# The last two down products of the second block exchanged, and the last row block finished in halves

## The chip, the cores and the metric

The kernel runs on one core of a Trainium2 chip. The core has TensorE for matrix products, VectorE, ScalarE and GpSimd for everything element by element, and SyncE, which issues most transfers; the profile calls them PE (PEld for its weight loads), DVE, ACT, POOL and SP. Each engine takes its instructions in order and waits for the others by semaphores. TensorE writes its sums into PSUM, eight banks of 128 x 512 float32 values; everything else lies in SBUF or in device memory. The metric is the device time of one execution in microseconds (us), as the median of several runs.

## The reference

The program is an encoder of two layers over 1024 tokens of width 1024. Each layer is a token mixer and a gated feed-forward block, each followed by a layer norm:

```python
for i in range(DEPTH):
    mix = _mla_mixer(h, ...) if i % 2 == 0 else _diff_mixer(h, ...)
    h = _layernorm(ALPHA * h + mix, ln_mix_g[i], ln_mix_b[i])
    h = _layernorm(ALPHA * h + _swiglu(h, ffn_w_gu[i], ffn_w_down[i]), ln_ffn_g[i], ln_ffn_b[i])

def _swiglu(x, w_gu, w_down):
    gate, up = jnp.split(x @ w_gu, 2, axis=-1)
    return (jax.nn.silu(gate) * up) @ w_down
```

The layer norm takes each row's mean and variance over its 1024 values, with the variance as the mean of the squares about the mean. Here only the last step matters: the product with `w_down` (2816 x 1024) of the second layer, the addition to the residual, and the last layer norm, whose result is the output.

## The kernel before

**The down product.** `ffn` (L486) computes the gated block for one layer; the second layer calls it with `next_x` None (L1388). The matrix product with `w_down` is done in Winograd's form of Strassen's scheme: rows are cut into two halves (row blocks 0 to 3 and 4 to 7, of 128 tokens each), columns into two halves of 512, the inner size into two halves of 11 blocks of 128, and seven products of half size take the place of eight. Each product pairs one of seven combinations of h, written to device memory earlier (`h_dr`), with a combination of weight quarters made on the fly. In the code's names, with the weights they use, the order before is b11, t1, b21, t2, b22, t3, t4 (L817 to L879). b11, b21 and b22 are quarters of the weights as loaded; t1 to t4 are differences, which VectorE subtracts first (for t4 at L769).

**One product** has 11 steps j. A step takes one 128 x 512 block of h and one of the weights, each split into a high part (ScalarE copies it, L469) and a low part (the difference, L470: VectorE for h, GpSimd for weights). `step` (L779) then issues three matmuls (high by high, high by low, low by high) for one row block t, so a whole product is 11 x 4 x 3 = 132 matmuls of 512 columns. `whole` (L787) goes over j outside and t inside.

**Banks.** Two sets of four PSUM banks are used in turn, `x4` and `y4`, one bank for each t. A product either begins anew in its banks or goes on adding to what is there: t3 adds onto t2, and t4 onto both, all in y4, because the scheme wants t2, t2 + t3 and t2 + t3 + t4. After each product `added` (L796, issued at L798) lets VectorE add the banks to the right quarter of the result z. A bank that is read there can be written by TensorE only when VectorE is done. b22 lies in x4, between t2 and t3.

**Operands.** Split blocks of h and of weights take their places in turn from three sets of slots, `wh` (3), `wl` (3) and `o` (6): twelve in all (`op_unit`, L474). Only t4 of this layer differs: its weights go to the eleven `tt` tiles (L775), which held the upper half of the raw weights until then, so that all of its h and weights can be kept. Raw h comes in groups of four blocks through two buffers (L725), raw weights in groups of four through larger ones; `load_down` (L715) keeps all these loads in the program's order on SP.

**The end before.** t4's steps go over row blocks 0 and 1 together, step by step; then come all eleven steps of row block 2, then those of row block 3 (L866 to L879). Behind each row block stand `added` and `finish`.

**The layer norm** (`layer_norm`, L163) of a row block: VectorE forms minus the mean in two scalings (L166, L167) from two sums that `added` collected; ScalarE squares both halves about the mean with a running sum (L170); VectorE centres and multiplies by the gain (L176); it adds the two sums of squares (L178); GpSimd raises that to -1/2 (L180); VectorE multiplies and adds the bias (L183); SP stores (L184). The very last row block does the final step and the store in two halves of 512 columns. Row blocks 4 to 7 are finished after b22, while TensorE works on t3.

**Order.** The lines above are in program order. A scheduler at build time takes that order as the priority, simulates the engines, and lays each engine's queue out from it; so an instruction that the simulation finds ready earlier can stand ahead of one that the program lists first. `behind` (L155) pins one instruction after another: t4's subtractions from the third on stand behind the last `added` before them (L771).

## Time and profile before

| | us |
|---|---|
| median of three runs | 2318.11 (2317.43 to 2320.41) |
| the profiled execution | 2317.24 |
| its span, first to last instruction | 2315.5 |
| VectorE busy in the span | 1560.1 |
| ScalarE busy in the span | 1018.5 |
| GpSimd busy in the span | 891.9 |

The profile is of one execution. Its page gives each engine's busy time and share; the other views are lists. In the timeline a row has the start in us from the span's beginning, the duration, the engine, the line of the kernel, the operation, the tiles (written <- read), the shape, how many were merged (x), and in brackets how long the engine sat idle before and what ended that. A matmul's duration includes the time in which it drains, so that matmuls overlap: their pace is the distance of starts. The view by windows has a row for each stretch: its length, then the busy time and number of instructions of PE, PEld, DVE, ACT and POOL, the clock granted to TensorE as a share of full speed, the share of time that the transfer engines were busy, and GB/s. Groups by line give busy time, the mean of one in ns, and idle time before. The chain lists the work that ended last, step by step. Tile names: op_h and op_w are split operands, wt the split weights in the tt tiles, dx, dy, dw and dv the banks of the products, z the result, fg and fb the gain and bias.

### The profile page before, as it was taken

The numbers are of one execution on the slowest core, as the hardware profiler recorded it, in microseconds if no ns is written. First come the engines' busy times: TensorE is split into PE (matmuls) and PEld (weight loads), VectorE is DVE, ScalarE is ACT, GpSimd is POOL, SyncE is SP. The second block draws the span as 40 slices with busy tenths as digits, with TensorE's granted clock in tenths as the row PEclk, the third lists the DMA queues.
The fourth block names the chain that finished last, engine by engine and source line by source line (L and its number), as shares of the span: only waits on it lengthen the run. The fifth ranks groups of instructions, "written<-read, shape, count | busy, mean of one in ns | idle before, by whom it ended". The sixth has DMA issues, their size and how long they took to land. (4 is left out here: it accounts for less than half of the span.)

```text
span 2315.5 us, 31126 instructions
## 1 busy us (share of the span) xinstructions
PE 2253.4 (97%) x11410; PEld 1918.7 (83%) x11410; DVE 1560.1 (67%) x2879; ACT 1018.5 (44%) x2092; POOL 891.9 (39%) x698
## 2 busy tenths in 40 slices
PE   9999999999999999999999999979999999999997
PEld 9898897888888887888888898967778888887886
DVE  5666664596666658677476766666596656658777
ACT  4466673352332324345465656545442333324343
POOL 2233351014444445465332423222014444436564
PEclk9999999999999999999999999989999999999999
DMA  5121335334323238454310202153344222337453
GB/s 202 41 91 69 106 101 178 125 142 145 125 76 129 86 119 322 182 183 140 101 46 31 71 25 69 37 191 111 126 144 149 99 103 102 113 129 303 146 203 121
DMA packets 103658, 288.29 MB, mean 125 GB/s; under 512 B 8528, under 2 KB 31696, under 8 KB 93008
## 3 DMA queue, kind: packets, MB, share of 16 engines
q1 hardware_dynamic: 98064, 268.46, 33.0%
q0 software_dynamic: 5440, 17.83, 2.3%
q8 instruction: 90, 1.47, 0.3%
q14 instruction: 64, 0.52, 0.1%
HBM read 205.00 MB, written 77.07 MB: 122 GB/s over the span
## 5 line engine op out<-in xcount | busy, mean ns | idle before, releaser
L469 ACT CAST op_g<-gr 128x512 fp32r<-128x512 f32 x240 | 147.5, 622 | 411.0 <-PE gb L514 228.3
L470 POOL TENSOR_TENSOR op_g<-gr,op_g 128x512 fp32r<-128x512 f32 x104 | 145.8, 1407 | 303.6 <-DVE tmp L605 153.6
L470 DVE TENSOR_TENSOR op_h<-rh,op_h 128x512 fp32r<-128x512 f32 x154 | 162.8, 1088 | 67.6 <-ACT op_h L469 67.6
L514 PE MATMUL ga<-xh_m,op_g 128*128 128x512 f32 x512 | 168.0, 389 | 0.0
L469 ACT CAST op_h<-rh 128x512 fp32r<-128x512 f32 x154 | 93.0, 619 | 145.0 <-PE dx L782 37.5
L782 PE MATMUL dw<-op_w_t,op_h 128*128 128x512 f32 x660 | 151.4, 390 | 0.0
L782 PEld LDWEIGHTS dw<-op_w_t,op_h 128*128 128x128 f32 x660 | 123.6, 188 | 25.9 <-DVE op_h L470 0.4
L222 ACT ACTIVATE l_b<-l_b,mx_b 128x256 f32<-128x256 f32 (+7 forms) x128 | 99.6, 778 | 76.2 <-DVE mx_b L219 74.2
L1281 POOL TENSOR_SCALAR l_b<-l_b,r_b,cst 128x128 f32<-128x128 f32 (+3 forms) x64 | 52.8, 825 | 205.1 <-DVE r_b L224 196.1
L470 POOL TENSOR_TENSOR op_w_t<-tt,op_w_t 128x512 fp32r<-128x512 f32 x66 | 98.8, 1501 | 77.1 <-ACT op_w_t L469 77.1
L782 PE MATMUL dx<-op_w_b,op_h 128*128 128x512 f32 x528 | 122.7, 392 | 5.9 <-ACT op_w_b L469 3.9
L782 PEld LDWEIGHTS dx<-op_w_b,op_h 128*128 128x128 f32 x528 | 98.3, 188 | 29.9 <-ACT op_w_b L469 4.7
L514 PE MATMUL gb<-t4h_f,op_g 128*128 128x512 f32 x352 | 115.8, 390 | 3.0 <-DVE tmp L597 3.0
L514 PE MATMUL gc<-b22h_f,op_g 128*128 128x512 f32 x352 | 115.6, 389 | 1.6 <-ACT op_g L469 1.6
L470 DVE TENSOR_TENSOR op_g<-gr,op_g 128x512 fp32r<-128x512 f32 x136 | 109.5, 807 | 9.0 <-ACT op_g L469 8.8
L514 PE MATMUL gc<-t1h_f,op_g 128*128 128x512 f32 x352 | 115.5, 389 | 0.0
L514 PE MATMUL gb<-t3h_f,op_g 128*128 128x512 f32 x352 | 115.2, 389 | 0.0
L514 PE MATMUL gb<-t2h_f,op_g 128*128 128x512 f32 x352 | 114.8, 389 | 0.0
L514 PEld LDWEIGHTS ga<-xh_m,op_g 128*128 128x128 f32 x512 | 96.1, 188 | 19.9
L470 POOL TENSOR_TENSOR op_g<-s,op_g 128x512 fp32r<-128x512 f32 x40 | 55.3, 1382 | 143.6 <-ACT op_g L469 143.6
L143 PE MATMUL bp<-xT_f,h_wb 128*128 128x512 f32 x256 | 103.4, 404 | 0.0
L145 PE MATMUL bp<-xT_f,l_wb 128*128 128x512 f32 x256 | 101.8, 398 | 0.0
(375 smaller groups left out, 6788.4 us busy)
## 6 DMA issues: line engine op xcount, KB each, us to landing
gr<-in_w_gu SPq DMA_DIRECT2D x44, 1024.0 KB, 6.7
rh<-h_dr SPq DMA_DIRECT2D x28, 1024.0 KB, 5.3
h_dr<-sh SPq DMA_DIRECT2D x22, 1024.0 KB, 4.9
h_dr<-hp SPq DMA_DIRECT2D x22, 768.0 KB, 4.1
tt<-in_w_dn SPq DMA_DIRECT2D x22, 512.0 KB, 7.5
rh<-h_dr SPq DMA_DIRECT2D x14, 768.0 KB, 4.3
z<-xs_dr SPq DMA_DIRECT2D x16, 512.0 KB, 10.0
rw_b<-in_w_dn SPq DMA_DIRECT2D x8, 1024.0 KB, 8.7
```

The lines of the kernel that those rows point to most:

```text
L143: T.matmul(ps_out, lh, rh, start=(i == 0), stop=False)
L145: T.matmul(ps_out, ll, rh, start=False, stop=(i == n - 1))
L222: A.activation(l[:, :n], l[:, :n], AF.Exp, bias=mx, scale=-1.0, accum_out=sm)
L469: A.copy(hi, src)
L470: eng.tensor_tensor(lo, src, f32(hi), ALU.subtract)
L514: T.matmul(o, w[:, a, kc], x[b][:, k, :], start=(first and k == 0 and (a, b) == (0, 0)), stop=(k == 3 and a == 1), skip_group_check=True,)
L782: T.matmul(o, h[:, a, c], w[:, b_], start=(first and (a, b_) == (0, 0)), stop=(last and a == 1), skip_group_check=True,)
L1281: G.tensor_scalar(l1[:, :n], l1[:, :n], r1, nlam, ALU.mult, ALU.mult)
```

## The change

In the second layer b22 moves from between t2 and t3 to the very end. The products now run b11, t1, b21, t2, t3, t4, b22: t2, t3 and t4 follow each other on y4, and t4 is an ordinary `whole` product whose weights take the common slots. Row blocks 0 to 3 are finished after t4; b22's split weights are put into the tt tiles, its steps go over row blocks 4 and 5 together, then 6, then 7, and each is finished behind its steps. For row block 7 the first half of the result is complete much earlier (after b21), and `last_row_block` squares that half about its own mean ahead of time; `end` squares the second half about the same mean and corrects by the square of the difference of the two means. It also centres the two halves separately, so that the second half's centring stands behind the request for the power -1/2, and writes the result in three stores: the first 512 columns by SP, the next 256 by ScalarE's queue, the last 256 by SP. `layer_norm` loses its parameter for halves. The first layer keeps its order (`third`).

```diff
-    def layer_norm(z, sums, junk, y, g, b, name, dst, n=1):
+    def layer_norm(z, sums, junk, y, g, b, name, dst):
...
-        for i in range(n):
-            c = slice(i * D // n, (i + 1) * D // n)
-            V.scalar_tensor_tensor(y[:, c], y[:, c], rs, b[:, c], ALU.mult, ALU.add)
-            nc.sync.dma_start(dst[:, c], y[:, c])
+        V.scalar_tensor_tensor(y, y, rs, b, ALU.mult, ALU.add)
+        nc.sync.dma_start(dst, y)
...
-                if next_x is not None:
-                    yield unit(r, f"t4_{j}", G, ("o",))
-                    continue
-                t = poolx.tile([P, 2, 512], F32R, tag=f"tt{j}", name=f"wt4{layer}_{j}")
+                yield unit(r, f"t4_{j}", G, ("o",)) if next_x is not None else unit(r, f"t4_{j}")
+
+        def b22_kept():
+            for j, r in enumerate(w_block(1, hi_half, "b22")):
+                t = poolx.tile([P, 2, 512], F32R, tag=f"tt{j}", name=f"wt{layer}_{j}")
                 split((t[:, 0], t[:, 1]), r, G)
                 yield t
...
+        def last_row_block(tb, o, junk):
+            s_lo, s_hi = (sums[tb][:, i:i + 1] for i in range(2))
+            nb, q = small(f"nb{layer}"), small(f"q{layer}")
+            sq, d, nmu, rs = (small(f"{k}{layer}", 2) for k in ("sq", "dm", "nm", "rs"))
+
+            def square(i, cs, to):
+                A.activation(to, z[tb][:, cs], AF.Square, bias=nb, scale=1.0 / 32, accum_out=sq[:, i:i + 1])
+
+            V.tensor_scalar(nb, s_lo, -1.0 / (32 * 512), None, ALU.mult)
+            square(0, lo_half, junk)
+            V.tensor_scalar(q, sq[:, 0:1], LN_EPS, None, ALU.add)
+
+            def end():
+                added(0, hi_half, o, tb - 4, 1)
+                square(1, hi_half, o)
+                V.tensor_scalar(nmu[:, 0:1], s_hi, s_lo, -1.0 / D, ALU.add, ALU.mult)
+                V.tensor_scalar(d[:, 0:1], s_hi, s_lo, 1.0 / D, ALU.subtract, ALU.mult)
+                V.tensor_scalar(d[:, 1:2], d[:, 0:1], d[:, 0:1], -1.0, ALU.mult, ALU.mult)
+                V.tensor_scalar(d[:, 1:2], d[:, 1:2], q, None, ALU.add)
+                y, dst = z[tb], x_dst[tb * P:(tb + 1) * P, :]
+                V.scalar_tensor_tensor(y[:, lo_half], y[:, lo_half], nmu[:, 0:1], g[:, lo_half], ALU.add, ALU.mult)
+                V.tensor_scalar(rs[:, 1:2], sq[:, 1:2], d[:, 1:2], None, ALU.add)
+                G.tensor_tensor(rs[:, 0:1], rs[:, 1:2], mhalf[:, 0:1], ALU.pow)
+                V.scalar_tensor_tensor(y[:, hi_half], y[:, hi_half], nmu[:, 0:1], g[:, hi_half], ALU.add, ALU.mult)
+                for cs, eng in ((lo_half, nc.sync), (slice(512, 768), nc.scalar), (slice(768, 1024), nc.sync)):
+                    V.scalar_tensor_tensor(y[:, cs], y[:, cs], rs[:, 0:1], b[:, cs], ALU.mult, ALU.add)
+                    eng.dma_start(dst[:, cs], y[:, cs])
+
+            return end
...
+        def third():
+            whole(x4, from_h(6, "3"), block(1, hi_half, "b22"), True)
+            for t in range(4):
+                added(0, hi_half, x4[t], t, 1)
+                finish(4 + t, [x4[t], x4[t]])
+
         x4 = accumulators("v", "x")
-        whole(x4, from_h(6, "3"), block(1, hi_half, "b22"), True)
-        for t in range(4):
-            added(0, hi_half, x4[t], t, 1)
-            finish(4 + t, [x4[t], x4[t]])
+        if next_x is not None:
+            third()
...
         if next_x is None:
+            whole(y4, from_h(2, "4"), t4(), False)
+            for t in range(4):
+                added(1, lo_half, y4[t], t, 0)
+                finish(t, [y4[t], y4[t]])
+            end = last_row_block(7, x4[3], y4[3])
             hs, ws = [], []
-            for h, w in zip(from_h(2, "4"), t4()):
+            for j, (h, w) in enumerate(zip(from_h(6, "3"), b22_kept())):
                 hs.append(h)
                 ws.append(w)
                 for t in range(2):
-                    step(y4[t], h, w, t, False, len(hs) == 11)
+                    step(x4[t], h, w, t, j == 0, j == 10)
+            for t in range(4):
+                if t > 1:
+                    for j in range(11):
+                        step(x4[t], hs[j], ws[j], t, j == 0, j == 10)
+                if t == 3:
+                    end()
+                else:
+                    added(0, hi_half, x4[t], t, 1)
+                    finish(4 + t, [x4[t], x4[t]])
             stx.close()
-            last(0)
-            last(1)
-            for t in range(2, 4):
-                for j in range(11):
-                    step(y4[t], hs[j], ws[j], t, False, j == 10)
-                last(t)
```

More of the change, by code (lines that the diff above doesn't have):

```diff
@@ L804, in finish @@
             y = z[tb] if y is None else y
-            return layer_norm(z[tb], sums[tb], junk, y, g, b, f"{nm}_{tb}", x_dst[tb * P:(tb + 1) * P, :],
-                              2 if next_x is None and tb == 3 else 1)
+            return layer_norm(z[tb], sums[tb], junk, y, g, b, f"{nm}_{tb}", x_dst[tb * P:(tb + 1) * P, :])
+        def last_row_block(tb, o, junk):
[23 more added lines that the diff above has]
+            return end
         def accumulators(name, tag):
@@ L859, in ffn @@
             added(1, hi_half, y4[t], t, 1)
-        def last(t):
-            added(1, lo_half, y4[t], t, 0)
-            finish(t, [y4[t], y4[t]])
         new, rest, normed = None, [], []
         if next_x is None:
+            whole(y4, from_h(2, "4"), t4(), False)
[3 more added lines that the diff above has]
+            end = last_row_block(7, x4[3], y4[3])
             hs, ws = [], []
-            for h, w in zip(from_h(2, "4"), t4()):
+            for j, (h, w) in enumerate(zip(from_h(6, "3"), b22_kept())):
                 hs.append(h)
```

## The prediction

> **What bounds the kernel now.** I read the page first, then the last four stages by window, then the timeline around the end, then the last part of the chain.
>
> ```profile
> span 2315.5 us, 31126 instructions
> PE 2253.4 (97%) x11410; PEld 1918.7 (83%) x11410; DVE 1560.1 (67%) x2879; ACT 1018.5 (44%) x2092; POOL 891.9 (39%) x698
> 2210.70:2240.80 30.10, 30.10 (x134) 24.74 (x133) 21.96 (x21) 15.41 (x28) 23.17 (x16) 1.00 0.46 167
> 2240.80:2270.80 30.00, 30.00 (x133) 24.59 (x131) 29.18 (x42) 18.36 (x38) 16.92 (x13) 1.00 0.59 210
> 2270.80:2303.80 33.00, 30.62 (x133) 24.62 (x132) 25.90 (x40) 11.88 (x23) 15.87 (x11) 1.00 0.18 65
> 2303.80:2315.50 11.70, 0.00 (x0) 0.00 (x0) 6.56 (x12) 1.87 (x6) 1.09 (x2) 0.71 0.34 135
> ```
>
> The program is bound by TensorE: 97% of the span, and in the three windows (one each for the b22, t3 and t4 products; the fourth is the tail) it is busy throughout, but for the last, where 33.00 us hold 30.62 of work. The tail, 11.70 us, has no matmul. So the change can save in two places only: the holes of the t4 product and the tail. Everything earlier in the program stays as it is. The profiled execution took 2317.24 us, its span and 1.74 around it; the median of the runs is 2318.11, 0.87 above it. I subtract from the median.
>
> The holes, in the timeline:
>
> ```profile
> 2244.66 26.23 PE L782 MATMUL dw<-op_w_t,op_h 128*128 128x512 f32 x115
> 2268.05 0.32 SPq L717 DMA_DIRECT2D rh<-h_dr  x1
> 2271.54 0.68 DVE L798 SCALAR_TENSOR_TENSOR z<-z,dw 128x512 f32<-128x512 f32 x1
> 2272.37 1.63 PE L782 MATMUL dw<-wt,op_h 128*128 128x512 f32 x6 [1.48 <-DVE z L798]
> 2272.83 1.66 ACT L469 CAST op_h<-rh 128x512 fp32r<-128x512 f32 x3 [6.19 <-DMA rh<-h_dr]
> 2273.48 0.69 DVE L470 TENSOR_TENSOR op_h<-rh,op_h 128x512 fp32r<-128x512 f32 x1 [1.25 <-ACT op_h L469]
> 2274.09 0.68 DVE L798 SCALAR_TENSOR_TENSOR z<-z,dw 128x512 f32<-128x512 f32 x1
> 2274.83 15.52 PE L782 MATMUL dw<-wt,op_h 128*128 128x512 f32 x67 [0.83 <-DVE z L798]
> 2289.74 13.99 PE L782 MATMUL dw<-wt,op_h 128*128 128x512 f32 x61
> ```
>
> The first row gives the pace: 115 matmuls in 26.23 us, the last taking 0.39, so (26.23 - 0.39) / 114 = 0.2267 us each, and 132 x 0.2267 = 29.92 per product. t3's last matmul ends at 2270.89, t4's at 2303.73: 32.84, so **2.92 us** were lost. t4 adds into the banks y4 that t3 filled, and VectorE must read a bank before TensorE writes it again. The read of the first bank (2271.54) and of the second (2274.09) came late because VectorE's queue held split operands of h ahead of them, and one of these waited for ScalarE's copy, which waited 6.19 us for an h load issued at 2268.05.
>
> The tail:
>
> ```profile
> 2299.00 0.69 DVE L798 SCALAR_TENSOR_TENSOR z<-z,dw 128x512 f32<-128x512 f32 x1 [0.33 <-PE dw L782]
> 2304.08 0.69 DVE z L798 x2
> 2304.69 1.28 DVE L176 SCALAR_TENSOR_TENSOR z<-z,nmu_f,fg 128x1024 f32<-128x1024 f32 x1
> 2306.01 0.21 DVE L166 TENSOR_SCALAR nmu_f<-fs 128x1 f32<-128x1 f32 x1
> 2306.13 0.21 DVE L167 TENSOR_SCALAR nmu_f<-fs 128x1 f32<-128x1 f32 x1
> 2306.25 0.69 ACT L170 ACTIVATE dw<-z,nmu_f 128x512 f32<-128x512 f32 x1 [2.21 <-DVE nmu_f L166]
> 2306.88 0.19 ACT L170 ACTIVATION_READ_ACCUMULATOR dw<-z,nmu_f 128x1 f32 x1
> 2306.76 1.28 DVE L183 SCALAR_TENSOR_TENSOR z<-z,rs_f,fb 128x1024 f32<-128x1024 f32 x1 [0.42 <-POOL rs_f L180]
> 2307.96 1.28 DVE L176 SCALAR_TENSOR_TENSOR z<-z,nmu_f,fg 128x1024 f32<-128x1024 f32 x1
> 2309.15 0.21 DVE L178 TENSOR_SCALAR ve_f<-ssq_f 128x1 f32<-128x1 f32 x1
> 2309.44 0.55 POOL L180 TENSOR_TENSOR rs_f<-ve_f,cst 128x1 f32<-128x1 f32 x1 [2.72 <-DVE ve_f L178]
> 2310.03 1.41 DVE L183 SCALAR_TENSOR_TENSOR z<-z,rs_f,fb 128x512 f32<-128x512 f32 x2 [0.66 <-POOL rs_f L180]
> 2310.80 0.99 SPq L184 DMA_DIRECT2D out_dram<-z  x2
> out_dram<-z SPq DMA_DIRECT2D x2, 256.0 KB, 2.0
> ```
>
> From the last matmul's end (2303.73) to the first of the final two VectorE halves (2310.03; call it F) are **6.30 us**; from F to the end of the span 5.47, of which 1.41 are the two halves and 2.0 the last store's landing. In the 6.30, VectorE still works off the row block before the last (2304.69, 2306.76: 1.20 us apart from their followers each), so that the last one's mean comes at 2306.01, 1.24 us after its sums (2304.08 + 0.69 = 2304.77), and its centring pass (2307.96) behind another wide pass.
>
> **Part 1: the products exchanged.** Before, b22 (other banks) lay between t2 and t3, and its 30 us hid VectorE's reads of t2's banks. Now t2, t3, t4 follow each other on y4, so there are two transitions on one bank, and t4 to b22 changes banks and needs no wait. Behind a late read all of TensorE stands. What such a transition costs is read where VectorE's order was undisturbed, at b22's end:
>
> ```profile
> 2224.72 16.25 PE L782 MATMUL dv<-op_w_b,op_h 128*128 128x512 f32 x71
> 2238.97 0.69 DVE L798 SCALAR_TENSOR_TENSOR z<-z,dv 128x512 f32<-128x512 f32 x1 [2.05 <-PE dv L782]
> 2239.58 1.77 DVE L470 TENSOR_TENSOR op_h<-rh,op_h 128x512 fp32r<-128x512 f32 x1
> 2241.27 0.68 DVE L798 SCALAR_TENSOR_TENSOR z<-z,dv 128x512 f32<-128x512 f32 x1
> 2242.13 0.67 DVE L798 SCALAR_TENSOR_TENSOR z<-z,dv 128x512 f32<-128x512 f32 x1
> 2242.73 0.67 DVE L798 SCALAR_TENSOR_TENSOR z<-z,dv 128x512 f32<-128x512 f32 x1
> ```
>
> b22's last matmul ends at 2240.97, so the next would start at 2240.81. Its reads end at 2239.66, 2241.95, 2242.80 and 2243.40. Had the next product used these banks, three matmuls (0.68) for each bank in turn: the first at 2240.81, the second held from 2241.49 to 2241.98, the third from 2242.66 to 2242.83, the fourth from 2243.51 not at all: 0.65 us, and the first six after a hole take 0.1 longer (1.63 at 2272.37, against 5 x 0.2267 + 0.39 = 1.52): **0.75** each, 1.5 for two. The bounds: 0 each when no operand is queued between the reads, 2.92 each as at the t4 product now. I take 1.5, since the h load that came late belonged to a product whose eleven weights had tiles of their own and whose h filled all slots ahead; now t3 loads no weights, t4's h and weights share twelve slots and are prepared six pairs ahead at most, and no finishes disturb VectorE in t3. The term: 2.92 - 1.5 = **1.4 us saved**.
>
> Moved with it are loads and stores on SP's queue. The h and weight loads of t4 come ahead of b22's; the stores of row blocks 0 to 3 follow t4, not 4 to 7 follow b22. SP waits for each store's operand in order, but b22's loads become issuable as t4's pairs are consumed, before any of these stores. t4's subtractions (L769) move a stage forward, out of the last one; they still stand behind t3's last read.
>
> b22's weights now go into the tt tiles, each free when t4's subtraction and t3's split have read it.
>
> ```profile
> L470 POOL TENSOR_TENSOR wt<-rw_t,wt 128x512 fp32r<-128x512 f32 x11 | 18.7, 1733 | 13.1 <-ACT wt L469 13.1
> L470 DVE TENSOR_TENSOR op_h<-rh,op_h 128x512 fp32r<-128x512 f32 x77 | 80.2, 1074 | 30.5 <-ACT op_h L469 30.5
> 2252.73 2.31 DVE L183 SCALAR_TENSOR_TENSOR z<-z,rs_f,fb 128x1024 f32<-128x1024 f32 x1 [0.20 <-POOL rs_f L180]
> 2251.61 0.68 DVE L470 TENSOR_TENSOR op_h<-rh,op_h 128x512 fp32r<-128x512 f32 x1
> 2251.76 0.93 POOL L180 TENSOR_TENSOR rs_f<-ve_f,cst 128x1 f32<-128x1 f32 x1 [1.29 <-DVE ve_f L178]
> ```
>
> GpSimd has 22 low parts to make for both products, 22 x 1.733 = 38.1 us, from some 4 us after t3's end (reads 2.4 as at b22's end, a copy 0.62, a subtraction of about 1): done 42 behind it and 12 into the last product, whose eleventh pair is needed 10 x 6 x 0.2267 = 13.6 in. That cover of 1.5 us hides it; without it TensorE waits for weights.
>
> **Part 2: VectorE in the last product.** It now holds four finishes (rows 0 to 3) and three more (4 to 6) before the last. One finish: its two wide passes 1.20 each, three column operations of 0.12, an add of 0.69: 3.45; seven are 24.2. The stage gives 29.92, and 5.7 are left. Into that fall the low parts of h that find no slot before t4 ends (two or three of 0.69 to 1.77, 2 to 5 us) and passes that run beside GpSimd (2.31 instead of 1.28, some four: 4 us). So VectorE is between 0 and 3.3 us behind at the last matmul; I take **1.0**.
>
> **Part 3: the last row block.** The first half's square, its mean and two column operations go ahead of the last matmul; ScalarE has 21 of 33 us free in that window (11.88 busy), which hides them; uncovered, the square would cost 0.82. After the last matmul's end: the add from 0.03 to 0.72. ScalarE squares the other half from 0.75 (0.82 from its start to the accumulator read's end, 2306.25 to 2307.07): done at 1.57. VectorE meanwhile: nmu at 0.72 and d at 0.84 (pace 0.12 by L166 and L167), then two that need the one before. No row shows such a pair; between 0.12 and 0.24 (0.21 and 0.03 to wake), I take 0.24. The first half's pass starts at 1.44 and takes 0.61 to the next (2304.08 to 2304.69), so rs is at 2.05: ScalarE is hidden. The power follows 0.29 behind (2309.15 to 2309.44), at 2.34, alone until 2.89. But the second half's pass runs from 2.17 to 2.86 beside it. Beside such an operation the power took 0.93 and ended 0.40 after it (2252.69 after 2252.29): 3.26. The page "SBUF — State Buffer" of the Trainium skill, section "SBUF: two separate sides", says that a VectorE operation with two SBUF inputs and a GpSimd one lock each other out for a whole instruction; by it the power would start at 2.86 and end at 3.41, and that speaks against laying these two beside each other. The trace's 0.40 agrees in kind, and the sum goes by it. F is at 3.26 + 0.04 = **3.30** instead of 6.30, 3.0 saved; less the 1.0 of Part 2, **2.0 us**.
>
> From F on: halves of 512, 256 and 256 columns instead of two of 512. A 256 is between 0.12 and 0.61, by the straight line 0.37; so 0.61 + 0.37 + 0.45 = 1.43 against 1.41. The middle store is issued by ScalarE, whose queue holds nothing behind it but the program's end; no row shows such an issue: it lands ahead of the last if it takes up to 2.3, and SP's took 2.0; had it the 2.6 of the 512 KB stores it would be 0.3 late. I take 0 for all of this.
>
> Sum: 1.4 + 2.0 = 3.4; 2318.11 - 3.4 = **2314.7 us** (2313.8 by the profiled execution).
>
> **The rivals.**
> *Both gains whole.* The reads come at once at both transitions and VectorE has caught up: 2.92 + 3.0 = 5.9, 2312.2. For it: nothing but the h load made t4's reads late. Against: at b22's end an operand stood between two reads anyway.
> *The hole twice.* Both transitions wait as the one does now: 2.92 lost instead of saved, 2.0 gained, 2319.0. For it: the one example in this stage. Against: its late load has gone.
> *VectorE bounds the end (the slower side).* The low parts of h for b22 are made in the last stage, not ahead: eleven of 1.074 are 11.8, with 24.2 and the 4 beside GpSimd 40.0, 10 more than the stage. F then comes at 13.3, 7.0 later than now; less 1.4, 5.6 slower: 2323.7. It decides from a backlog of 4.4 us (3.0 + 1.4) on. For it: the four finishes in t3's window kept VectorE busy 29.18 of 30.00 us beside such parts. Against: b22's h need no slots that t4 doesn't free.
>
> **How the numbers follow.** A measurement of this kernel can tell about 0.2% (4.6 us) from no change. The forecast has 0.42 (2313 to 2317), the whole gain 0.27, the hole twice 0.16, VectorE's bound 0.15. Faster by over 0.2% (under 2313.5) is the second and 0.05 of the first: 0.32; slower (over 2322.7) is the last: 0.15; the rest 0.53. The range 2311.8 to 2320.0 leaves out the last case and 0.05 at the edges of the others.
>
> **What would show it.** Matmuls from t2's end to the last without a hole over 0.7 us: Part 1. The last add within 0.1 us of the last matmul's end, and no other row block's pass behind it: Part 2. F 3.3 us behind that end, the power near 0.9 us: Part 3. I am wrong if TensorE waits in the last product for weights, or if a hole of over 1 us stands at a transition, or if two passes of row block 6 follow the last matmul.

## The result, and the profile after

The changed kernel takes **2326.27 us** (median of 9 runs, 2324.29 to 2332.39); the kernel before, run beside it, 2319.53. The ratio is 1.0031, its 95% interval 1.0021 to 1.0042: some 7 us slower. The profiled execution took 2325.18 us, with a span of 2323.4.

The first lines of the changed kernel's page:

```profile
span 2323.4 us, 31155 instructions
PE 2252.8 (97%) x11410; PEld 1916.3 (82%) x11410; DVE 1554.9 (67%) x2885; ACT 1017.8 (44%) x2092; POOL 887.8 (38%) x698
```

Its windows over b22's product (now the last) and the tail:

```profile
2271.30:2304.88 33.58, 32.66 (x134) 24.04 (x132) 30.70 (x48) 17.24 (x38) 16.75 (x13) 1.00 0.30 116
2304.88:2323.40 18.52, 0.00 (x1) 0.00 (x0) 12.20 (x27) 4.07 (x10) 2.19 (x4) 0.58 0.29 114
```

TensorE's work is the same to 0.6 us (2252.8 against 2253.4). b22's 33.58 us hold 32.66 of matmuls, and the tail has grown from 11.70 to 18.52 us. These 6.8 us are most of the 7.9 by which the span of this execution is longer (2323.4 against 2315.5); the other 1.1 is a later last matmul. In the tail VectorE is busy 12.20 us where it was 6.56.

The timeline of TensorE in the changed kernel, from t2's end to the last matmul:

```profile
2204.80 5.15 PE L781 MATMUL dw<-op_w_t,op_h 128*128 128x512 f32 x22
2211.35 60.26 PE L781 MATMUL dw<-op_w_t,op_h 128*128 128x512 f32 x264 [1.40 <-DVE z L797]
2271.45 13.34 PE L781 MATMUL dv<-wt,op_h 128*128 128x512 f32 x49
2285.51 19.38 PE L781 MATMUL dv<-wt,op_h 128*128 128x512 f32 x83 [0.72 <-POOL wt L468]
```

One hole stands between t2 and t3 (it waits for z, VectorE's read of a bank). t3 and t4 then run as one block of 264 matmuls, and b22 follows without a gap. But inside b22, 49 matmuls take 13.34 us where the pace allows 48 x 0.2267 + 0.39 = 11.27, and a hole follows. The last matmul ends at 2304.88.

VectorE (DVE) and the loads on SP's queue of the changed kernel, from the end of t4's subtractions to the first finish:

```profile
2254.62 1.78 DVE L767 TENSOR_TENSOR rw_t<-rw_t,tt 128x512 f32<-128x512 f32 x1
2256.33 5.29 DVE L468 TENSOR_TENSOR op_h<-rh,op_h 128x512 fp32r<-128x512 f32 x5
2259.84 0.32 SPq L715 DMA_DIRECT2D rh<-h_dr  x1
...
2270.13 1.58 DVE L468 TENSOR_TENSOR op_h<-rh,op_h 128x512 fp32r<-128x512 f32 x1 [8.51 <-ACT op_h L467]
...
2282.42 0.67 DVE L797 SCALAR_TENSOR_TENSOR z<-z,dw 128x512 f32<-128x512 f32 x1
...
2285.69 0.68 DVE L797 SCALAR_TENSOR_TENSOR z<-z,dw 128x512 f32<-128x512 f32 x1
...
2287.19 2.31 DVE L176 SCALAR_TENSOR_TENSOR z<-z,nmu_f,fg 128x1024 f32<-128x1024 f32 x1
```

The first h load for b22 is issued only at 2259.84. SP keeps the loads in order and has to wait for one of the two buffers of raw h; that buffer is free when VectorE has made t4's operands from it, and these stand on VectorE's queue behind t4's subtractions (the last at 2254.62). So VectorE sits idle for 8.51 us until 2270.13: it waits for ScalarE's copies of b22's operands. These begin with the weights, whose load SP issues right behind that h load, and so they are late as well:

```profile
POOL wt L468 <- ACT wt L467: 11.9, 2, 9.3
ACT wt L467 <- DMA rw_b<-in_w_dn: 11.6, 2, 10.8
```

These two rows are waits between 2200 and 2306, with the us in total, how many there were and the longest: ScalarE waited 11.6 us for b22's raw weights, and GpSimd 11.9 us for ScalarE's copies of them. Then, on VectorE, the low parts of b22's h come first, t4's four sums only from 2282.42 to 2285.69, and the first wide pass of a finish at 2287.19: 15.6 us after TensorE was done with t4 (2211.35 + 60.26).

VectorE's group of h operands between 2270 and 2305 in the changed kernel, from the view by line:

```profile
L468 DVE TENSOR_TENSOR op_h<-rh,op_h 128x512 fp32r<-128x512 f32 x11 | 14.6, 1384 | 8.5 <-ACT op_h L467 8.5
```

And its window from the first of them to the first column operation of a finish:

```profile
2270.13:2284.84 14.71, 14.45 (x56) 9.59 (x54) 14.71 (x13) 8.98 (x18) 12.14 (x8) 1.00 0.42 154
```

All eleven low parts of b22's h are made from 2270.13 on, and none is done when the last product starts (2271.45): 14.6 us. VectorE is busy without any pause from 2270.13 to 2284.84.

The end of the changed kernel's timeline:

```profile
2307.09 0.68 DVE L797 SCALAR_TENSOR_TENSOR z<-z,dv 128x512 f32<-128x512 f32 x1
...
2314.36 0.68 DVE L797 SCALAR_TENSOR_TENSOR z<-z,dv 128x512 f32<-128x512 f32 x1
...
2317.39 0.55 POOL L830 TENSOR_TENSOR rs<-rs,cst 128x1 f32<-128x1 f32 x1 [4.26 <-DVE rs L829]
2317.97 1.54 DVE L833 SCALAR_TENSOR_TENSOR z<-z,rs,fb 128x512 f32<-128x512 f32 x3 [0.73 <-POOL rs L830]
```

The sum of row block 6 is taken at 2307.09, 2.2 us after the *last* matmul of the program; that of row block 7 at 2314.36, 9.5 us after its data were there. From there to F are 3.61 us. F, the start of the last row block's final pieces, now stands 13.09 us behind the last matmul instead of 6.30. From F (2317.97) to the end of the span are 5.43 us, against 5.47.

**Theories.** The reading leaves three. *Theory 1:* the loads for b22 come late, and a third buffer for raw h would mend it. *Theory 2:* VectorE has too much to do in the last product whatever the loads do: four finishes that used to lie in the stage before, and b22's operands. *Theory 3:* the new end for the last row block is at fault.

### The profile page after: what moved, and what is told of

Its sections match the earlier page's. It is cut to its first block, busy times and chain, and to the rows that moved or that the text cites. A ratio compares the mean times of both kernels' runs of the same rounds, so it can differ in the third digit from the quotient of the medians.

```text
span 2323.4 us, 31155 instructions
## 1 busy us (share of the span) xinstructions
PE 2252.8 (97%) x11410; PEld 1916.3 (82%) x11410; DVE 1554.9 (67%) x2885; ACT 1017.8 (44%) x2092; POOL 887.8 (38%) x698
## 4 chain that ended last, share of the span: by engine, by line
PE 85%; DVE 7%; DMA 3%; issue 2%; ACT 2%; POOL 0%; SPq 0%; DVEq 0%; POOLq 0%; ACTq 0%
PE gb L512 15%; PE gc L512 10%; PE ga L512 9%; PE dw L781 5%; PE zp_a L387 4%; PE s_a L214 3%; PE s_b L214 3%; PE dx L781 3%; PE bp L143 3%; PE bp L144 3%; PE bp L145 3%; PE dy L781 2%; PE o_a L253 2%; PE o_b L253 2%; DVE op_h L468 2%
## 5 line engine op out<-in xcount | busy, mean ns | idle before, releaser
L468 DVE TENSOR_TENSOR op_h<-rh,op_h 128x512 fp32r<-128x512 f32 x154 | 157.0, 1049 | 81.5 <-ACT op_h L467 81.5
L781 PE MATMUL dw<-op_w_t,op_h 128*128 128x512 f32 x792 | 181.3, 390 | 1.4 <-DVE z L797 1.4
L781 PEld LDWEIGHTS dw<-op_w_t,op_h 128*128 128x128 f32 x792 | 148.2, 188 | 32.8 <-ACT op_w_t L467 1.8
```

The costliest lines, as they stand in the source:

```text
L468: eng.tensor_tensor(lo, src, f32(hi), ALU.subtract)
L781: T.matmul(o, h[:, a, c], w[:, b_], start=(first and (a, b_) == (0, 0)), stop=(last and a == 1), skip_group_check=True,)
```

## The experiments

All were timed in five rounds against the kernel before, each beside it on the same chip (e1 to e8 on one, e9 to e12 on another). Times are medians in us. A profile is of one execution, and where its earlier stages run early or late, everything behind them moves along: the kernels' b21 products start between 2148.72 and 2157.30. Distances inside the end are safer than times from the start.

| run | change | time | before | ratio (95%) |
|---|---|---|---|---|
| e1 | after, third raw buffer | 2324.29 | 2319.32 | 1.0019 (1.0008 to 1.0029) |
| e2 | after, old end | 2329.3 | 2319.32 | 1.0049 (1.0033 to 1.0064) |
| e3 | before, third raw buffer | 2318.27 | 2319.32 | 0.9998 (0.9989 to 1.0006) |
| e4 | before, new end | 2318.71 | 2319.32 | 1.0003 (0.9992 to 1.0014) |
| e5 | after, no finishes 0 to 3 | 2316.58 | 2318.31 | 0.9994 (0.9985 to 1.0002) |
| e6 | after, no low h for b22 | 2325.63 | 2318.31 | 1.0028 (1.0018 to 1.0038) |
| e7 | after, last weights on VectorE | 2322.42 | 2318.31 | 1.0020 (1.0011 to 1.0029) |
| e8 | before, last weights on VectorE | 2323.13 | 2318.31 | 1.0022 (1.0013 to 1.0030) |
| e9 | before, finishes 4 to 7 late | 2323.94 | 2318.39 | 1.0022 (1.0013 to 1.0031) |
| e10 | e7 and e1 together | 2320.39 | 2318.39 | 1.0012 (1.0003 to 1.0020) |
| e11 | before, last product eased | 2318.74 | 2318.39 | 0.9998 (0.9989 to 1.0006) |
| e12 | e11 with two orders mended | 2317.38 | 2319.13 | 0.9994 (0.9982 to 1.0005) |

### e1: a third buffer for raw h in the changed kernel

```diff
-        poolh = ...tile_pool(name=f"fh{layer}", bufs=2, ...)
+        poolh = ...tile_pool(name=f"fh{layer}", bufs=2 if next_x is not None else 3, ...)
```

> The changed kernel with a third buffer for raw groups of h in the second layer, nothing else. Late loads: b22's first raw h can be issued right behind t4's (near 2238 instead of 2259.84), its low parts are made as slots come free, VectorE reads t4's banks at t4's end (near 2272 instead of 2282 to 2286), the backlog at the last matmul falls from 9.5 us to under 3, and the time to about 2316 (10 us under the changed kernel). Too much work for VectorE in the last product, whatever the loads: seven finishes and eleven low parts still stand there, the backlog stays over 7 us and the time within 3 us of 2326.

It moved the first load, and hardly the time. The timelines of SP, VectorE and TensorE in e1:

```profile
2240.68 0.32 SPq L715 DMA_DIRECT2D rh<-h_dr  x1
...
2257.79 12.54 DVE L468 TENSOR_TENSOR op_h<-rh,op_h 128x512 fp32r<-128x512 f32 x8
2262.96 0.32 SPq L715 DMA_DIRECT2D rh<-h_dr  x1
...
2274.50 2.77 DVE L468 TENSOR_TENSOR op_h<-rh,op_h 128x512 fp32r<-128x512 f32 x2 [4.17 <-ACT op_h L467]
2276.29 30.08 PE L781 MATMUL dv<-wt,op_h 128*128 128x512 f32 x132
```

The first loads for b22 go out at 2240.68, 19 us sooner, and b22 runs without a hole (132 matmuls in 30.08 us). Yet only two of b22's eleven low parts are made ahead: of the eight from 2257.79 six are t4's own, held up behind its nine subtractions. The other nine still come after 2274.50, and the sums of t4 after them. The reason is the second of b22's three groups of h. It still goes out only at 2262.96 (2261.64 in the changed kernel), since its buffer waits for t4's operands, and the raw weights behind it are late with it: ScalarE waits 7.73 us for them, and VectorE for ScalarE (the 4.17). Besides, GpSimd now makes four of b22's weights before the last of t4's, and TensorE stands 1.53 us for these in t4. The gain is 2 us, and the intervals of the two ratios overlap. So a third buffer doesn't mend the late loads; what loads wholly on time would give isn't shown by it.

### e2: the old end in the changed kernel

```diff
-            end = last_row_block(7, x4[3], y4[3])
...
-                if t == 3:
-                    end()
-                else:
-                    added(0, hi_half, x4[t], t, 1)
-                    finish(4 + t, [x4[t], x4[t]])
+                added(0, hi_half, x4[t], t, 1)
+                finish(4 + t, [x4[t], x4[t]])
```

> The products exchanged alone: the last row block is finished by the plain layer norm in two halves with two stores, as before. VectorE late from elsewhere: the same backlog, and from the last add to the final halves some 4.3 us instead of 3.6, so 0.7 us slower than the changed kernel, about 2327. The new end at fault: back at about 2319 to 2320.

Slower by another 3 us. The last sum and F of e2:

```profile
2316.86 0.68 DVE L799 SCALAR_TENSOR_TENSOR z<-z,dv 128x512 f32<-128x512 f32 x1
2321.72 1.42 DVE L183 SCALAR_TENSOR_TENSOR z<-z,rs_f,fb 128x512 f32<-128x512 f32 x2 [0.73 <-POOL rs_f L180]
```

From the last sum to F are 4.86 us where the new end takes 3.61, with no other row block in the way in either. Here the sum also comes later behind the last matmul (2306.14): 10.72 us instead of 9.48, so that more than the expected 0.7 was lost. The medians lie 3 us apart, though the intervals of the two ratios overlap. Theory 3 falls: without the new end nothing is won back.

### e3: a third buffer in the kernel before

The edit is that of e1.

> The kernel before with a third buffer for raw groups of h in the second layer. A late h load made the hole of 2.92 us between t3 and t4: the hole falls under 1 us and the time by about 2, to 2317.5. The reads of the banks are late for another reason (low parts that stand between them, VectorE's work in t3): the hole stays over 2 us and the time within 1 us of before.

No change can be told. Around the hole between t3 and t4, in e3:

```profile
2269.81 2.49 DVE L470 TENSOR_TENSOR op_h<-rh,op_h 128x512 fp32r<-128x512 f32 x4
2272.22 0.68 DVE L798 SCALAR_TENSOR_TENSOR z<-z,dw 128x512 f32<-128x512 f32 x1
2273.05 1.16 PE L782 MATMUL dw<-wt,op_h 128*128 128x512 f32 x4 [1.53 <-DVE z L798]
```

The h load is no longer late, and the hole is still there: VectorE's read of the first bank (2272.22) stands behind four low parts that are simply ahead of it in its queue (from 2269.81). Counted as in before (t3's last matmul's end to t4's, less 29.92) the loss is 2.19 us where it was 2.92. The prediction had named both the order on VectorE and the late load of 2268.05; the order alone makes most of it.

### e4: the new end in the kernel before

```diff
+            end = last_row_block(3, y4[3], x4[3])
...
-                last(t)
+                if t == 3:
+                    end()
+                else:
+                    last(t)
```

`last_row_block` is that of the change with the halves' parts exchanged, since here the second half is complete first.

> The order of products before, with the new end for its own last row block (3): the upper half, complete after t3, squared ahead about its own mean, three stores. Part 3 right and the row block ahead of it still in VectorE's queue: from the last matmul's end to the final pieces 4.8 to 5.3 us instead of 6.30, the time 1 to 1.5 us under before, about 2318.3. The new end at fault: slower than before.

No change can be told, although the end is 3 us shorter on paper, and the 4.8 to 5.3 us that were expected from the last matmul to F are 6.36. VectorE's timeline in e4, whose last matmul ends at 2305.15:

```profile
2305.51 0.68 DVE L798 SCALAR_TENSOR_TENSOR z<-z,dw 128x512 f32<-128x512 f32 x1
2306.12 1.28 DVE L176 SCALAR_TENSOR_TENSOR z<-z,nmu_f,fg 128x1024 f32<-128x1024 f32 x1
...
2309.14 1.28 DVE L183 SCALAR_TENSOR_TENSOR z<-z,rs_f,fb 128x1024 f32<-128x1024 f32 x1
...
2311.51 1.54 DVE L833 SCALAR_TENSOR_TENSOR z<-z,rs,fb 128x512 f32<-128x512 f32 x3 [0.73 <-POOL rs L830]
```

Between the last sum (2305.51) and F (2311.51) stand both wide passes of the row block before (2306.12 and 2309.14). From the sum to F it takes 6.00 us, as the old end did in before (2304.08 to 2310.03, 5.95). VectorE is busy with two row blocks there, so a shorter chain for one of them gives nothing.

### e5: the changed kernel without four finishes

```diff
-                finish(t, [y4[t], y4[t]])
+                nc.sync.dma_start(x_dst[t * P:(t + 1) * P, :], z[t])
```

> The changed kernel without the layer norms of row blocks 0 to 3: their sums are added and z is stored as it is, so this part of the output is left out. VectorE loses four times two wide passes (1.20 each) and three column operations (0.12), 11 us, from the last product, where it ends 9.5 us behind the last matmul. Theory 2 (too much work for VectorE in the last product): the backlog is gone, the power-of-minus-half step stands some 3.6 us behind the last matmul instead of 13.1, about 2317 us. Theory 1 (b22's loads come late): the loads and the holes in b22 stay as they are, so 2324 to 2326.

As Theory 2 expected to half a us: 2316.58. Its profiled execution took 2323.84, with t3 beginning 7.7 us later than in the changed kernel for a reason ahead of these stages that the median doesn't share; distances inside the end can be read all the same. TensorE's last block and VectorE's end in e5:

```profile
2297.02 16.18 PE L781 MATMUL dv<-wt,op_h 128*128 128x512 f32 x70 [0.77 <-DVE op_h L468]
2313.24 0.69 DVE L797 SCALAR_TENSOR_TENSOR z<-z,dv 128x512 f32<-128x512 f32 x1 [0.37 <-PE dv L781]
...
2316.79 1.54 DVE L833 SCALAR_TENSOR_TENSOR z<-z,rs,fb 128x512 f32<-128x512 f32 x3 [0.66 <-POOL rs L830]
```

The last sum comes 0.04 us after the last matmul's end (2313.20), and F 3.59 after it. b22's loads are as late as ever and its holes are still there. Without these four finishes the backlog of 9.5 us is gone, late loads and all.

### e6: the changed kernel without b22's low parts of h

```diff
-        split((t[:, 0], t[:, 1]), src, eng)
+        [A.copy(t[:, i], src) for i in range(2)] if name.startswith("h1_3_") else split((t[:, 0], t[:, 1]), src, eng)
```

> The changed kernel with VectorE's subtractions for b22's h left out: ScalarE copies the high part a second time in their place, so the low parts of this product are not computed. All matmuls, loads and finishes stay. The eleven took 1.1 to 1.77 us each on VectorE, 15 us between 2270 and 2287. Theory 2: without them the finishes begin as soon as t4's sums are there; the backlog of 9.5 us is gone and the time is about 2317. Theory 1: the loads come at 2260 to 2277 as before, ScalarE waits for them in VectorE's place, and the time stays at 2324 or more.

No gain, and the trace says that the experiment doesn't settle what it was made for. VectorE and ScalarE (ACT) in e6:

```profile
2274.17 0.68 DVE L797 SCALAR_TENSOR_TENSOR z<-z,dw 128x512 f32<-128x512 f32 x1
2286.94 0.69 ACT L170 ACTIVATE dw<-z,nmu_f 128x512 f32<-128x512 f32 x1
2289.53 1.40 DVE L176 SCALAR_TENSOR_TENSOR z<-z,nmu_f,fg 128x1024 f32<-128x1024 f32 x1 [14.67 <-ACT dw L170]
```

t4's sums are now taken by 2274.85, 11 us sooner. Then VectorE idles 14.67 us: the first finish needs ScalarE's squares, and these stand on ScalarE's queue at 2286.94, behind the copies for b22. Eleven of these were added here, and all start only at 2270.79, when ScalarE has waited 11.26 us for the raw weights; from there to the squares it is busy without a pause. So the finishes start as late as before, for another reason. It speaks for an end that hangs on when the first finish starts, not on how full VectorE is before that.

### e7: b22's weights on VectorE

```diff
-                split((t[:, 0], t[:, 1]), r, G)
+                split((t[:, 0], t[:, 1]), r, V)
```

> The changed kernel with the low parts of b22's weights made by VectorE in place of GpSimd; nothing is left out. If what makes VectorE slow in the last product is GpSimd beside it (its 512-column operations are 1.70 us apart there, 0.60 alone), 22 of them take 13.2 us on VectorE instead of eleven in 18.7: the backlog falls from 9.5 by 5.5 us, about 2320. If it is the mere number of instructions on the bounding engine, eleven more cost 0.60 to 1.07 each: 6.6 to 11.8 us more, 2333 to 2338.

Adding eleven instructions to the engine that bounds the end made the kernel no slower: the ratio falls by 0.0011, some 2.5 us, with intervals that overlap. VectorE's groups by line in e7, from 2268 to the last matmul:

```profile
L468 DVE TENSOR_TENSOR wt<-rw_b,wt 128x512 fp32r<-128x512 f32 x11 | 7.1, 683 | 7.3 <-ACT wt L467 7.3
L468 DVE TENSOR_TENSOR op_h<-rh,op_h 128x512 fp32r<-128x512 f32 x11 | 7.0, 683 | 0.0
```

TensorE's block for b22, and F, in e7's timeline:

```profile
2271.51 30.08 PE L781 MATMUL dv<-wt,op_h 128*128 128x512 f32 x132
2314.23 1.54 DVE L833 SCALAR_TENSOR_TENSOR z<-z,rs,fb 128x512 f32<-128x512 f32 x3 [0.73 <-POOL rs L830]
```

Twenty-two low parts take 7.1 + 7.0 = 14.1 us; the eleven beside GpSimd took 14.6. The page "SBUF — State Buffer" of the Trainium skill, section "SBUF: two separate sides", says that a VectorE operation with two SBUF inputs and a GpSimd one that reads SBUF shut each other out of a shared port for a whole instruction; the means of 683 ns here and 1384 there agree. b22 now has no hole, and TensorE ends at 2301.59, 2.1 us sooner than in before. Of these, 0.7 stand already where b21's product starts (2149.95 against 2150.64); the other 1.45 are what the exchange gives TensorE when nothing holds b22 up. But F is still 12.64 us behind, with all seven finishes there. The expectation's first reading, a backlog shorter by 5.5 us, therefore missed too: the last sum comes 7.62 us behind the last matmul instead of 9.48, and F only 0.45 sooner. What was gained, TensorE gained.

### e8: t4's weights on VectorE in the kernel before

The same edit in `t4`.

> The kernel before with the low parts of t4's weights (the last product's) made by VectorE in place of GpSimd; nothing is left out. By the theory of GpSimd slowing VectorE, the last product's queue on VectorE is 5 us shorter, row blocks 0 and 1 are added some 3 us sooner, and their finishes no longer stand in the way of the last one: the last row's chain of 6.3 us shrinks to 4 to 6, so 1 to 2 us less than before, about 2318. If it is the number of instructions, 6.6 us or more are added to VectorE's queue and the time is the same or up to 4 us longer.

Slower by 5 us, so both readings of the expectation missed. TensorE after the hole in e8's timeline:

```profile
2284.68 20.56 PE L782 MATMUL dw<-wt,op_h 128*128 128x512 f32 x80 [4.67 <-DVE wt L470]
```

A window of e8 from there on:

```profile
2284.68:2289.11 4.43, 4.43 (x11) 3.48 (x11) 4.43 (x8) 0.04 (x1) 0.00 (x0) 0.50 0.00 0
```

In this order VectorE also has t4's nine subtractions, and the scheduler put all of them ahead of the third weight's low part, the first that is made in this stage. TensorE stood 4.67 us for it, and then ran at a granted clock of 0.50 for 4.43 us. The work was cheap, its place in the queue wasn't.

### e9: the finishes of before moved into the last product

```diff
-            finish(4 + t, [x4[t], x4[t]])
+            if next_x is not None:
+                finish(4 + t, [x4[t], x4[t]])
...
+        if next_x is None:
+            for t in range(4):
+                behind(finish(4 + t, [x4[t], x4[t]])[1], banks_read[-1])
```

> The kernel before, products in its own order, but the finishes of row blocks 4 to 7 held back until t3's sums are read, so that they fall into the last product; nothing is left out. It is the price of four finishes there by itself, without the exchange, without late loads and with the old end. Four finishes are 11.0 us of VectorE's work; in the last product of before it is busy 25.6 of 32.7 us, so 7.1 fit and 4 to 6 remain behind the last matmul: 2322 to 2325. If the exchange itself (b22's loads and operands) is what costs, this kernel stays at 2318 to 2319.

The counter-test to e5, and inside what was expected: 2323.94, 5.6 us slower than before, with no products exchanged. A window of e9 over the last product:

```profile
2271.00:2305.23 34.23, 31.25 (x137) 25.23 (x135) 25.27 (x50) 13.75 (x31) 21.54 (x13) 1.00 0.16 63
```

Two of VectorE's groups by line in that window, with the idle time before them:

```profile
L176 DVE SCALAR_TENSOR_TENSOR z<-z,nmu_f,fg 128x1024 f32<-128x1024 f32 x5 | 7.9, 1571 | 3.2 <-ACT dv L170 3.2
L183 DVE SCALAR_TENSOR_TENSOR z<-z,rs_f,fb 128x1024 f32<-128x1024 f32 x4 | 5.0, 1281 | 5.7 <-POOL rs_f L180 5.7
```

TensorE's last block and F in e9's timeline:

```profile
2281.36 23.87 PE L782 MATMUL dw<-wt,op_h 128*128 128x512 f32 x104 [2.98 <-POOL wt L470]
...
2316.44 1.41 DVE L183 SCALAR_TENSOR_TENSOR z<-z,rs_f,fb 128x512 f32<-128x512 f32 x2 [0.72 <-POOL rs_f L180]
```

F is 11.21 us behind the last matmul (2281.36 + 23.87), where it was 6.30. The last matmul comes 1.5 us later than in before, but 1.1 of this stand already at t3's start (2241.95 against 2240.81): the old holes between t3 and t4 are gone, and TensorE stood 2.98 us for a weight from GpSimd instead. VectorE isn't full in this window: it waits 5.7 us for GpSimd's powers (GpSimd makes the low parts of weights in the same stretch, busy 21.54 us) and 3.2 for ScalarE's squares. A finish is a chain through three engines, and what counts is how much of such chains is left when the matmuls end. So the expected number came out, though not by the expected way of a full VectorE. Theory 2 holds as far as the four finishes go, with this addition.

### e10: both easings of the changed kernel

> The changed kernel with b22's weights' low parts on VectorE and a third buffer for raw h; nothing is left out. With the weights on VectorE the time was 2322.4 and VectorE sat idle for 7.3 us just before b22, waiting for loads, while it ended 11 us late. If the third buffer brings these loads ahead, 3 to 4 us of the idle time are used: about 2319. If the slots for split operands and not the buffer hold b22's h back, it is worth no more than the 2 us it was worth alone: 2320 to 2322.

2320.39, which is what the second reading allowed: together the two easings take 4 to 5 us off the changed kernel (ratio 1.0012 against 1.0031, intervals apart), and it is still slower than before. The edit is that of e1 and that of e7.

### e11 and e12: can the last product of before be eased

In both, t4's weights are split by VectorE, each of t4's subtractions from the sixth on is pinned behind the low part of three weights earlier (which mends e8), and the new end of e4 is there, its sum pinned behind row block 2's finish.

```diff
+                if j > 4:
+                    behind(i, lows[j - 3])
...
-                split((t[:, 0], t[:, 1]), r, G)
+                split((t[:, 0], t[:, 1]), r, V)
+                lows.append(low[0])
...
             def end():
                 added(1, lo_half, o, tb, 0)
+                behind(banks_read[-1], low[0])
```

> The kernel before in its own order of products, with VectorE's queue eased where the runs so far show it to bind: the low parts of t4's weights on VectorE, each pinned three subtractions behind its own so that TensorE isn't starved; the last three h operands of t4 pinned behind t3's reads; the last row block's end in halves, its add pinned behind row block 2's finish. Nothing is left out. Row blocks 0 and 1 should be added at 2290 instead of 2293.8, the hole between t3 and t4 shrink from 2.9 to about 1, and the last final pieces start 3.6 us after the last matmul instead of 6.3: 3 to 4.5 us in all, 2314 to 2316. If the mere number of VectorE's instructions counts, 2319 or more.

No change can be told, where 2314 to 2316 were expected. (The pin on t4's last h operands did not take hold in e11: it fell on the weights' low parts.) VectorE in e11, from the last weight to the first sum:

```profile
2288.00 1.90 DVE L470 TENSOR_TENSOR wt<-rw_t,wt 128x512 fp32r<-128x512 f32 x3
2295.85 0.69 DVE L806 SCALAR_TENSOR_TENSOR z<-z,dw 128x512 f32<-128x512 f32 x1 [5.95 <-PE dw L790]
```

All weights are ready at 2289.9, but row block 0 is complete only 6 us later, since TensorE's queue mixes in the early steps of row blocks 2 and 3. e12 mends that (matmuls of row blocks 2 and 3 from the fourth step on are pinned behind row block 1's last) and pins the low parts of h from the fifth on behind the weight's of two steps earlier.

```diff
+                    if next_x is None and name == "4" and j > 3:
+                        behind(low[0], lows[j - 2])
...
-                    step(y4[t], hs[j], ws[j], t, False, j == 10)
+                    step(y4[t], hs[j], ws[j], t, False, j == 10, mm if j > 2 else None)
```

> The kernel before in its own order of products, eased as in the last run but with two orders mended that its trace showed at fault: TensorE takes row blocks 0 and 1 through all steps before row blocks 2 and 3 go beyond the third step (there their sums came at 2295.8, 6 us after the last weight was ready), and the low parts of h from the fifth on stand two weights behind instead of ahead of t3's reads. Nothing is left out. If what keeps the last row block waiting is that three finishes begin too late, rows 0 and 1 are added at 2292, row 2's finish is out of the way by 2304, and the final pieces start 3.6 us after the last matmul instead of 6.3 to 7.5: 2314 to 2315. If VectorE has too much to do in any order, 2318 as before.

VectorE's end in e12, whose last matmul ends at 2302.45:

```profile
2291.15 0.69 DVE L810 SCALAR_TENSOR_TENSOR z<-z,dw 128x512 f32<-128x512 f32 x1 [1.75 <-PE dw L791]
...
2303.66 1.28 DVE L183 SCALAR_TENSOR_TENSOR z<-z,rs_f,fb 128x1024 f32<-128x1024 f32 x1 [0.73 <-POOL rs_f L180]
2304.86 0.68 DVE L810 SCALAR_TENSOR_TENSOR z<-z,dw 128x512 f32<-128x512 f32 x1
...
2308.47 1.54 DVE L846 SCALAR_TENSOR_TENSOR z<-z,rs,fb 128x512 f32<-128x512 f32 x3 [0.73 <-POOL rs L843]
```

With the low parts of h out of the way of the reads, t4 follows t3 without a hole (t3 starts at 2240.55, t4 at 2270.47, one product of 29.92 later); in e11, without this pin, TensorE still waits 1.14 us there. So the order on VectorE makes the old hole. TensorE ends 1.3 us sooner than in before (0.3 of them from earlier stages), rows 0 and 1 are added at 2291.15, and yet F is 6.02 us behind: row block 2's last pass (2303.66) still stands before the last sum. The expected 2314 to 2315 were missed: the median of e12 is 1.75 us below before's, but the interval (0.9982 to 1.0005) includes no change. No version here is shown to beat the kernel before.

## Why the prediction was wrong, step by step

**The step that failed is Part 2**, and with it the sentence in Part 1 on which it rests. Part 2 counted as b22's operands in the last product only "the low parts of h that find no slot before t4 ends (two or three of 0.69 to 1.77, 2 to 5 us)", and took a backlog of 1.0 us. It was eleven, 14.6 us, and the backlog 9.5. All three signs of being wrong that the prediction named stand in the trace: TensorE waits 0.72 us for a weight in the last product, 1.40 us at a transition, and both of row block 6's wide passes (2311.03 and 2313.16) follow the last matmul. Part 1 said that "b22's loads become issuable as t4's pairs are consumed". They became issuable when VectorE had worked through t4's subtractions and then the raw h in the buffer (2259.84). With the third buffer (e1) nine of the eleven were late all the same, for t4's own operands were.

A second term of Part 2 stood at nothing: the waits inside the chain of finishes. From the first wide pass (2287.19) to the last sum (2314.36) are 27.17 us, in which VectorE is busy 22.66; for the other 4.5 it waits for GpSimd's powers and ScalarE's squares. From the first wide pass to F it takes 30.8 us in the changed kernel, 29.8 in e1, 28.6 in e6, 29.4 in e7 and 29.7 in e10, nearly the same each time, and about as long as a whole product. So whatever holds up the first finish behind t4's last matmul comes out at the end: 15.6 us in the changed kernel, 8.8 in e10, the fastest of these five.

**The size of the four finishes** was in the sum (24.2 us for seven), and its place was known. What was missing is how little room was left for it: e5 and e9 price four finishes in the last product at 9.7 us (2326.27 to 2316.58, or 8.6 by the ratios) and 5.6 us. The forecast let all seven fit into the product with 5.7 us to spare, and the operands alone took more than twice that.

**The rival on the slower side is what happened**, nearly to its numbers: F at 13.3 was worked out, 13.09 measured. It gave 5.6 us more; 6.7 were measured between the medians, 7.9 between the spans. The rest is in b22's holes: the last matmul ends at 2304.88 instead of 2301.59 (e7), which the rival didn't have. That its backlog of 10 us met the 9.5 is in part luck: the operands took 14.6 instead of 11.8, the waits 4.5 instead of nothing, passes beside GpSimd 1.0 (one of 2.31) instead of 4, and the product was 33.3 us long instead of 29.9. Its chance of 0.15 was too small. What was set against it, "b22's h need no slots that t4 doesn't free", is true and beside the point: slots came free, but the order on VectorE's queue and the raw buffers decided.

**Part 1, the transitions.** 0.75 for each of two was expected. t2 to t3 cost more (1.56 us: 1.79 from start to start, less one pace), t3 to t4 next to nothing (the block of 264 matmuls is 0.25 us longer than the pace gives); 1.8 against 1.5 together, so the term of 1.4 saved was about right; e7 shows 1.45. It was lost again inside b22. The late load, given as one cause of the old hole, is a small part of it (2.19 of the 2.92 us stay in e3). The cover of 1.5 us over GpSimd's weights didn't hold, but not because GpSimd had too much to do: it waited 11.9 us for weights that were loaded late, and TensorE's hole at 2285.51 ends with 0.72 us for such a weight. In e1, where GpSimd makes the same low parts, b22 has no hole.

**Part 3, the end.** From the last sum to F 3.27 us were expected, 3.61 and 3.55 (e5) measured. The difference is an order: the scheduler put the second half's pass ahead of the last two column operations, so the power came alone and took 0.55 instead of 0.93, but started at 3.03 us after the sum instead of 2.31. The 3.0 us "saved", however, exist only where the row block before is finished. In the order of before they are nothing (e4). In the changed order the new end is 1.25 us shorter from the last sum to F (e2). From F on, 0 was taken and 0.04 less found.

**What stays open.** That the four finishes cost the time where they now lie is shown from both sides (e5, e9). How much of the 6.7 us the low parts of h alone cost isn't settled, since e6 put ScalarE's queue in their place; nor is what loads on time would give, since the second group of them stayed late in e1 and e10 (2262.96 and 2260.64). e7 only says that some 2.5 us of it are GpSimd's doing, if that.

## What to carry to other kernels

When a stage is moved to the end, list what its neighbours used to hide: here the finishes of the *other* half changed places with it, and lost a whole product's time to hide in. Count an engine's work in the last stage by where its queue lets each piece start, through every engine that the piece passes, not by free slots or by the stage's spare time. And before a tail is shortened, look whether the engine in it is busy with the row before; if so, a shorter chain for the last row gives nothing by itself (e4).

## What the runs showed of the hardware

Two things were not expected. The low part of a 512-column operand takes VectorE 0.68 us with GpSimd quiet and up to 1.78 beside it, so that taking GpSimd's work over can cost VectorE nothing (14.1 us for 22 in e7, 14.6 for eleven). And a hole of 4.67 us in TensorE's work was followed by 4.43 us at half the granted clock (0.50, e8), while one of 2.98 us was followed by none (e9: 1.00 over the whole product). The page "TensorE: Matmul & The Clock Gate" of the Trainium skill, section "Part 1: The HAM clock gate", puts the fall to half speed behind an idle window of about 3.4 us; both rows agree with it.
